# The expert layers of a streaming encoder: half of u and all values written as a software pipeline that three engines keep in program order

## The chip, the cores and the metric

One core of one Trainium2 chip runs the whole program as one launch. The metric is the device time of that launch in microseconds (us). Before the change it is 2491.96 us, the median of 3 runs (2488.18 to 2493.15).

Names of engines: TensorE (PE in the profile, its weight loads PEld), VectorE (DVE), ScalarE (ACT), GpSimd (POOL), and SyncE (SP), which only issues loads here.

## The reference

The program is one step of an encoder with two layers, a state-space mixer and an attention mixer, each followed by the same kind of expert layer ("peer"). There are 256 prompt rows and 8 x 16 = 128 sample rows. The change touches the expert layer alone, which runs twice:

```python
def peer(xn, w_q, sub_k1, sub_k2, u_tab, v_tab):
    ...
        vs, ci = lax.top_k(cand, PEER_TOPK)
        e1 = jnp.take_along_axis(i1, ci // PEER_TOPK, axis=-1)
        e2 = jnp.take_along_axis(i2, ci % PEER_TOPK, axis=-1)
        eid = (e1 * PEER_NKEYS + e2).reshape(PEER_TOKEN_BLOCK, PEER_HEADS * PEER_TOPK)
        gate = jax.nn.softmax(vs.astype(jnp.float32), axis=-1).reshape(PEER_TOKEN_BLOCK, PEER_HEADS * PEER_TOPK)
        ue = jnp.take(u_tab, eid, axis=0)
        act = jax.nn.gelu(jnp.einsum('tkd,td->tk', ue, xb).astype(jnp.float32))
        ve = jnp.take(v_tab, eid, axis=0)
        return jnp.einsum('tk,tkd->td', (gate * act).astype(xb.dtype), ve)
```

The table has 128 x 128 = 16384 experts of 1024 numbers each, u and v. A row picks 8 x 16 = 128 of them, with a gate for each.

## The kernel before

**Prompt rows, dense.** The 256 prompt rows use the whole table. The experts are cut into 128 blocks of 128, and a loop runs over blocks twice: first all of u, then all of v ("values"). The results of u are kept in two tiles, G[0] (blocks 0 to 63) and G[1] (blocks 64 to 127), as gelu(u x). Between u and values each entry of G is multiplied by its gate, or by zero.

**One step of u** (`u_step`) loads a block of 512 KB (tile `raw`), splits it into a rounded part `hi` (ScalarE, L111) and a rest `lo` (VectorE, L112), makes 24 matmuls of 256 columns (8 slices of the contraction times hi*xhi, hi*xlo, lo*xhi, L147 to L149), and takes the gelu of the bank on ScalarE. In the first half some blocks skip the split and are multiplied in full precision; in the second half (steps 64 to 127, the part that the change touches) none does.

**One step of values** (`v_step`) loads and splits a block of v in the same way, splits the slice of G into `phi` and `plo`, and makes 12 matmuls of 512 columns (L160): 2 row blocks, 2 halves, and hi*phi, lo*phi, hi*plo. 12 of the first 64 steps ("native": 3, 8, 13 up to 58) multiply the raw block by G itself (L1292). All 128 steps add into four banks.

**Gates** (`w_step`) make the gate matrix of 8 rows of tokens and one half of the experts: VectorE builds two one-hot tiles and scales one (`ob` L1258, `og` L1261, `oa` L1274), ScalarE builds the other `oa` (L1271, L1272), 16 small matmuls join them in a bank (L1278), and VectorE multiplies G by the bank (L1280). 32 such steps treat G[0] during the second half of u, and 32 treat G[1] during the first half of values; each stands at every second step.

**Sample rows, gathered.** The 128 sample rows use gathered rows of the table instead. GpSimd gathers 512 KB for each of 128 u items (L1139 into `gath`, three buffers, two items ahead), and VectorE multiplies and sums each (`u_item`, L1179). Their number by the step is set by the table `U_DUE`. For v, three sample groups of four are summed on TensorE: 24 "quads", each of four gathered tiles in a free part of G, a small tile `cm` from VectorE (L1230), and 8 matmuls in source, 16 in the trace (L1236); `V_DUE` sets their steps: 6 during u, 10 in the first half of values, 8 in the second. The fourth group is summed by VectorE, 32 items (L1204, `I_DUE`), in values.

**What sets the order.** Nothing in the expert layer is ordered by hand, but for instructions marked by `pin`, which keep their order among themselves (u items, quads). The framework's scheduler works out the order of all others for each engine from its own model of the durations and from the order in which the code records them. Each engine then runs its own list strictly in that order, and waits at an instruction whose inputs or buffers aren't ready.

**Buffers.** `raw` has 4. `hi` and `lo` have 2 in the second half of u and 3 in values, until the last few steps (2). `phi` and `plo` have 3. TensorE's 8 banks: 2 hold the sample sums, 4 the prompt sums (values only).

## Time and profile before

| what | before |
|---|---|
| median of 3 runs | 2491.96 us |
| the profiled execution | 2509.09 us |
| its span, first to last instruction | 2507.4 us |
| granted TensorE clock, mean | 0.986 |
| ScalarE, VectorE, GpSimd busy share | 50%, 78%, 30% |
| HBM read | 630.62 MB |

The profiled execution is some 0.7% slower than the median, so a difference that is worked out from the trace is scaled by 2491.96/2509.09. "Idle before" in a row is how long the engine waited just before that instruction, with what ended the wait. Matmuls overlap: one of 512 columns is shown with 0.40 us, but the next starts 0.23 us after it, so times of TensorE are read from start to start. A few per cent of its records are missing (a group of 48 may show 42).

### The profile page before, as it was taken

What the parts mean: (1) busy time and instruction counts of PE and PEld (TensorE: products, weight loads), DVE (VectorE), ACT (ScalarE), POOL (GpSimd) and SP (SyncE); (2) the same over time, 40 slices, a digit from 0 to 9 for tenths busy, and PEclk for the clock granted to TensorE, in tenths of its full rate; (3) what the DMA queues carried; (4) which work ended last, traced back from release to release, by engine and by line L of the source; (5) the groups of instructions that cost most, each with busy time, mean ns of one, the idle gap of its engine ahead of it and who ended that gap; (6) DMA issues with size and microseconds to landing.
All of it is one profiled execution on the core that took longest, in us unless ns stands there. A gap on an engine that the chain in (4) does not pass through costs nothing.

```text
span 2507.4 us, 44188 instructions
## 1 busy us (share of the span) xinstructions
PE 2399.9 (96%) x16431; PEld 2022.1 (81%) x16432; DVE 1951.7 (78%) x4217; ACT 1241.9 (50%) x2406; POOL 741.3 (30%) x779
## 2 busy tenths in 40 slices
PE   8999999999999999998999998999999999998998
PEld 7899978999988886656776778999998886656776
DVE  5888846979887888868875676978987897878965
ACT  5655524433465665553444554433465565554443
POOL 2222200012323224455442100012334224456441
PEclk9999999999999999999999999999999999999999
DMA  5545434467789889999895424467789888999995
GB/s 196 178 172 197 147 127 150 144 224 272 267 305 329 289 292 345 339 345 376 335 364 188 137 81 153 148 214 256 270 307 337 286 296 330 334 369 367 333 364 203
DMA packets 177080, 649.75 MB, mean 259 GB/s; under 512 B 21136, under 2 KB 23040, under 8 KB 174208
## 3 DMA queue, kind: packets, MB, share of 16 engines
q1 hardware_dynamic: 99936, 365.85, 40.8%
q0 software_dynamic: 76928, 281.07, 31.2%
q8 instruction: 129, 2.11, 0.3%
q14 instruction: 87, 0.71, 0.1%
HBM read 630.62 MB, written 18.06 MB: 259 GB/s over the span
## 4 chain that ended last, share of the span: by engine, by line
PE 68%; DVE 6%; issue 4%; ACT 2%; DMA 2%; POOL 1%; another core or an unknown queue 1%; POOLq 0%; SPq 0%; DVEq 0%; ACTq 0%
PE bank L160 23%; PE bank L149 10%; PE bank L147 9%; PE bank L148 9%; PE bank L1236 4%; PE bank L1245 4%; PE bank L1292 3%; PE bank L1278 3%; DVE lo L112 2%; DVE gath L1179 1%; ACT hi L111 1%; DMA gath<-in_p_u,eidU 1%; DMA h<-hd 1%; POOL G L1139 1%
## 5 line engine op out<-in xcount | busy, mean ns | idle before, releaser
L111 ACT CAST hi<-raw 128x1024 fp32r<-128x1024 f32 (+1 forms) x479 | 496.9, 1040 | 535.2 <-PE bank L148 349.8
L112 DVE TENSOR_TENSOR lo<-raw,hi 128x1024 fp32r<-128x1024 f32 (+1 forms) x479 | 579.5, 1212 | 191.1 <-ACT hi L111 165.1
L1139 POOL DMA_INDIRECT gath<-in_p_u,eidU x256 | 317.4, 1240 | 898.5 <-DVE gath L1179 486.6
L149 PE MATMUL bank<-xhi,lo 128*128 128x256 f32 (+1 forms) x1344 | 405.0, 302 | 8.0 <-DVE lo L112 6.9
L147 PE MATMUL bank<-xhi,hi 128*128 128x256 f32 (+1 forms) x1344 | 403.6, 301 | 0.6 <-ACT hi L111 0.3
L148 PE MATMUL bank<-xlo,hi 128*128 128x256 f32 (+1 forms) x1344 | 397.5, 296 | 0.2 <-issue 0.2
L1139 POOL DMA_INDIRECT G<-in_p_v,eidT x192 | 214.8, 1119 | 198.8 <-PE bank L1236 138.4
L111 ACT CAST phi<-G 128x256 fp32r<-128x256 f32 x232 | 93.8, 405 | 360.7 <-PE bank L160 317.5
L149 PEld LDWEIGHTS bank<-xhi,lo 128*128 128x128 f32 x1344 | 254.6, 189 | 16.5 <-DVE lo L112 8.5
L147 PEld LDWEIGHTS bank<-xhi,hi 128*128 128x128 f32 x1344 | 254.7, 190 | 13.8 <-issue 5.7
L148 PEld LDWEIGHTS bank<-xlo,hi 128*128 128x128 f32 x1344 | 254.8, 190 | 1.0 <-issue 0.7
L147 PE MATMUL bank<-qhi,hi 128*128 128x256 f32 (+1 forms) x792 | 244.4, 309 | 8.9 <-ACT xf L935 7.3
L149 PE MATMUL bank<-qhi,lo 128*128 128x256 f32 (+1 forms) x792 | 239.0, 302 | 2.6 <-DVE lo L112 2.6
L148 PE MATMUL bank<-qlo,hi 128*128 128x256 f32 (+1 forms) x792 | 238.8, 302 | 0.0
L160 PE MATMUL bank<-lo,phi 128*128 128x512 f32 x640 | 206.5, 403 | 7.9 <-DVE lo L112 5.8
L160 PE MATMUL bank<-hi,phi 128*128 128x512 f32 x640 | 198.9, 409 | 12.1 <-ACT hi L111 8.9
L1271 ACT ACTIVATE oa<-ioh,e2T 128x128 f16<-128x128 f16 x512 | 163.3, 390 | 90.0 <-PE bank L1278 70.1
L160 PE MATMUL bank<-hi,plo 128*128 128x512 f32 x640 | 203.4, 398 | 0.2 <-issue 0.2
L112 DVE TENSOR_TENSOR plo<-G,phi 128x256 fp32r<-128x256 f32 x232 | 97.7, 422 | 103.0 <-PE bank L160 94.8
L160 PEld LDWEIGHTS bank<-hi,phi 128*128 128x128 f32 x640 | 117.4, 188 | 61.1 <-ACT hi L111 18.2
L1179 DVE SCALAR_TENSOR_TENSOR gath<-gath,xg 128x1024 f32<-128x1024 f32 x128 | 155.3, 1213 | 9.6 <-DMA gath<-in_p_u,eidU 9.5
L147 PEld LDWEIGHTS bank<-qhi,hi 128*128 128x128 f32 x792 | 151.4, 191 | 10.4 <-ACT xf L935 7.8
(371 smaller groups left out, 5045.3 us busy)
## 6 DMA issues: line engine op xcount, KB each, us to landing
raw<-in_u_t SPq DMA_DIRECT2D x256, 512.0 KB
raw<-in_p_v SPq DMA_DIRECT2D x256, 512.0 KB
raw<-in_w_in SPq DMA_DIRECT2D x32, 512.0 KB
raw<-in_p_w_q SPq DMA_DIRECT2D x32, 512.0 KB
raw<-in_w_z SPq DMA_DIRECT2D x16, 512.0 KB
s<-in_state_ssm SPq DMA_DIRECT2D x8, 1024.0 KB
out_sm_ssm<-s SPq DMA_DIRECT2D x8, 1024.0 KB
raw<-in_w_out SPq DMA_DIRECT2D x16, 512.0 KB
```

The lines of the kernel that those rows point to most:

```text
L111: act.copy(hi, raw)
L112: dve.tensor_tensor(lo, raw, hi32, op=OP.subtract)
L147: pe.matmul(ps, whi[:, s], xhi[:, k, c0:c1], start=(k == 0), stop=False)
L148: pe.matmul(ps, whi[:, s], xlo[:, k, c0:c1], start=False, stop=False)
L149: pe.matmul(ps, wlo[:, s], xhi[:, k, c0:c1], start=False, stop=(k == KD - 1))
L160: mm = pe.matmul(ps, x, w[:, hf * n:(hf + 1) * n], start=s_, stop=e_)
L1139: pool.indirect_dma_start(out=tile_, out_offset=None, in_=tab, in_offset=bass.IndirectOffsetOnAxis(ap=idx, axis=0))
L1179: pin(dve.scalar_tensor_tensor(tile_, tile_, 1.0, xg[g], op0=OP.mult, op1=OP.mult, accum_out=au[g][:, j:j + 1]))
L1236: pin(pe.matmul(out_s[hf][32 * q:32 * q + 32, :], cm[:, q], rows[q][:, hf * 512:hf * 512 + 512], start=(r == 0), stop=(r == 31), tile_posi ...
L1245: pe.matmul(ps, raw[:, k * P:(k + 1) * P], xf[:, k], start=(k == 0), stop=(k == KD - 1))
L1271: act.activation(a[:, i], ioh, AF.Square, scale=-1.0, bias=e2T[:, t, 0:1])
L1278: pe.matmul(ps[:, i0 + i], a[:, i], eg[:, i0 + i, j], start=(j == 0), stop=(j == 1))
```

## The change

The second half of u and all of values are recorded in another order, and the instructions of TensorE, VectorE and ScalarE that are recorded there are chained: each one must come after the one recorded before it on the same engine (`in_order`). Loads and gathers (SyncE and GpSimd) are not chained. Steps are taken apart: weights are split one step ahead in u and two in values, the gelu of a step is recorded behind the split of a later one, and a gate step is spread over three steps (prepare, matmuls, multiply). Gate steps start at steps 0, 1, 3, 5 and so on, at 61/32 steps from one to the next, up to 59 (`w_at`), in place of 1, 3, up to 63. `phi` and `plo` keep 3 buffers, one of them in another pool. The residual `h` is loaded back two steps earlier, and the extra `hi`/`lo` buffer is given up there. The numbers and kinds of instructions are the same.

```diff
+AHEAD = 2 * 64 - 8
...
+    @contextmanager
+    def in_order():
+
+        traced = nc.cur_bb.bb.instructions
+        n, last = len(traced), {}
+        for i in traced:
+            last[i.engine] = i
+        kind = mybir.DependencyInfo(mybir.DependencyClass.NoSync, mybir.DependencyReason.DATA)
+        yield
+        for i in traced[n:]:
+            if i.engine in HELD:
+                if i.engine in last:
+                    tc.add_manual_dep(i, last[i.engine].name, kind, reason="in order")
+                last[i.engine] = i
...
+            def w_apply(hf, t0, ones, eg):
+
+                ps = bank([P, 8, HE])
+                for i in range(8):
+                    for j in range(2):
+                        pe.matmul(ps[:, i], ones[i // 4][:, i % 4], eg[:, i, j], start=(j == 0), stop=(j == 1))
+                return hf, t0, ps
...
+            def v_acts(e2):
+
+                if e2 in NATIVE_V:
+                    return None
+                n = turn_of["v"] = (turn_of.get("v", -1) + 1) % 3
+                pl, bufs = (vpool, 2) if n else (one, 1)
...
+                return split(phi, plo, G[e2 // HE][:, e2 % HE])
...
+            w_at = {(61 * i) // 32: 8 * i for i in range(32)}
+            made, mult, gelu = [], [], []
+
+            def gates(hf, e2):
+                if made:
+                    mult.append(w_apply(*made.pop()))
...
+            wt = u_weights(HE)
+            held = in_order()
+            held.__enter__()
             for e2 in range(HE):
-                u_step(HE + e2)
-                tick(HE + e2)
-                if e2 % 2 == 1:
-                    w_step(0, 8 * (e2 // 2))
+                if mult:
+                    w_mult(*mult.pop())
+                nxt = u_weights(HE + e2 + 1) if e2 < HE - 1 else v_weights(0)
+                if gelu:
+                    u_gelu(*gelu.pop())
+                if e2 == HE - 1:
+                    ph = v_acts(0)
+                gelu.append((HE + e2, u_products(HE + e2, wt)))
+                wt = nxt
+                gates(0, e2)
                 if e2 >= 7:
                     quads(HE + e2)
+                if e2 in w_at:
+                    made.append(w_prep(0, w_at[e2]))
+                tick(HE + e2)
+            u_gelu(*gelu.pop())
...
             for e2 in range(2 * HE):
-                v_step(e2)
+                if mult:
+                    w_mult(*mult.pop())
+                while n < 2 * HE and n <= e2 + (2 if n < AHEAD else 1):
+                    if n == AHEAD:
+                        more.clear()
+                    wt = v_weights(n)
+                    stage.append((wt, v_acts(n)))
+                    n += 1
+                v_products(e2, *stage.pop(0))
                 if e2 == 35:
                     load_group(3)
+                gates(1, e2)
+                quads(2 * HE + e2)
+                if e2 in w_at:
+                    made.append(w_prep(1, w_at[e2]))
                 tick(2 * HE + e2)
                 item_tick(2 * HE + e2)
-                if e2 < HE and e2 % 2 == 1:
-                    w_step(1, 8 * (e2 // 2))
-                quads(2 * HE + e2)
-                if e2 == 2 * HE - 7:
-                    more.clear()
+                if e2 == AHEAD - 1:
                     lent.__exit__(None, None, None)
                     h = open_h()
                     pool.dma_start(h, spill)
+            held.__exit__(None, None, None)
```

What moves on the engines is seen at three places of layer 0. The first is TensorE in values, about step 50, where a quad (`cm`) stands. Before:

```order
L1236 MATMUL bank_7299<-G_622_3973,cm_12474 32x512
L160 MATMUL bank_10553<-lo_12543,phi_12546 128x512
L160 MATMUL bank_10554<-lo_12543,phi_12546 128x512
L160 MATMUL bank_10553<-hi_12542,plo_12547 128x512
L160 MATMUL bank_10554<-hi_12542,plo_12547 128x512
L160 MATMUL bank_10555<-lo_12543,phi_12546 128x512
L160 MATMUL bank_10556<-lo_12543,phi_12546 128x512
L160 MATMUL bank_10555<-hi_12542,plo_12547 128x512
L160 MATMUL bank_10556<-hi_12542,plo_12547 128x512
L1236 MATMUL bank_7299<-G_622_3973,cm_12474 32x512
L1236 MATMUL bank_7300<-G_622_3973,cm_12474 32x512 x4
```

The same engine and place now, where L1309 are the gate matmuls (L1278 before), L1253 the quad and L177 the products:

```order
L1309 MATMUL bank_12533<-og_12501,oa_12509 128x64
L1253 MATMUL bank_7299<-G_622_3973,cm_12550 32x512 x4
L1253 MATMUL bank_7300<-G_622_3973,cm_12550 32x512 x4
L177 MATMUL bank_10583<-hi_12479,phi_12483 128x512
L177 MATMUL bank_10584<-hi_12479,phi_12483 128x512
```

Before, one quad was cut into pieces with products between them; now its 8 matmuls stand together behind a step's products and gate matmuls.

The second is VectorE about step 58 of values, near the end of the gate steps. Before:

```order
L1258 TENSOR_TENSOR ob_12578<-ioh_76,e1T_3965 128x512
L1280 SCALAR_TENSOR_TENSOR G_1195_7294<-bank_12508,G_1195_7294 128x64x8
L1261 TENSOR_TENSOR og_12580<-ob_12578,g_619_3967 128x1024
L1274 TENSOR_TENSOR oa_12596<-ioh_76,e2T_3966 128x512
L112 TENSOR_TENSOR lo_12701<-raw_12698,hi_12700 128x1024
L1258 TENSOR_TENSOR ob_12657<-ioh_76,e1T_3965 128x512
L1280 SCALAR_TENSOR_TENSOR G_1195_7294<-bank_12577,G_1195_7294 128x64x8
L1261 TENSOR_TENSOR og_12659<-ob_12657,g_619_3967 128x1024
L1274 TENSOR_TENSOR oa_12675<-ioh_76,e2T_3966 128x512
```

Now (L129 is `split`, L1315 the multiply, L1282 to L1300 the preparation, L1196 the u item, L1221 the v item, L1247 the small tile of a quad):

```order
L1315 SCALAR_TENSOR_TENSOR G_1195_7294<-bank_12691,G_1195_7294 128x64x8
L129 TENSOR_TENSOR lox_12714<-raw_12711,hix_12713 128x1024
L129 TENSOR_TENSOR plo_12718<-G_622_3973,phi_12717 128x256
L1247 SCALAR_TENSOR_TENSOR cm_12733<-iob_74,a_10196 128x128
L1282 TENSOR_TENSOR ob_12745<-ioh_76,e1T_3965 128x512
L1285 TENSOR_TENSOR og_12747<-ob_12745,g_619_3967 128x1024
L1300 TENSOR_TENSOR oa_12755<-ioh_76,e2T_3966 128x512
L1196 SCALAR_TENSOR_TENSOR gath_12633,au_12246<-gath_12633,G_622_3973 128x1024
L1221 SCALAR_TENSOR_TENSOR G_622_3973<-G_622_3973,cU_3964 128x1024
```

Before, gate steps that had been put off followed each other with few splits between them; now each step holds at most one gate step's preparation and one multiply, behind the split of the weights.

The third is ScalarE in the second half of values. Before:

```order
L111 CAST phi_13247<-G_1195_7294 128x256
L111 CAST hi_13243<-raw_13241 128x1024
L111 CAST phi_13274<-G_1195_7294 128x256
L111 CAST phi_13299<-G_1195_7294 128x256
L111 CAST hix_13270<-raw_13268 128x1024
L111 CAST phi_13326<-G_1195_7294 128x256
```

Now:

```order
L128 CAST phi_13220<-G_1195_7294 128x256
L128 CAST hi_13241<-raw_13239 128x1024
L128 CAST phi_13245<-G_1195_7294 128x256
L128 CAST hi_13263<-raw_13261 128x1024
L128 CAST phi_13267<-G_1195_7294 128x256
L128 CAST hix_13290<-raw_13288 128x1024
```

Before, two or three `phi` of later steps stood ahead of the `hi` of a nearer one; now `hi` and `phi` of the same step take turns, `hi` first.

More of the change, by code (lines that the diff above doesn't have):

```diff
@@ L26 @@
 NSEQ = 8
+HELD = (mybir.EngineType.PE, mybir.EngineType.DVE, mybir.EngineType.Activation)
 TS = 16
@@ L1275, in w_step, with w_mult @@
                                           e2T[:, ts].unsqueeze(2).to_broadcast([P, 4, P // 2, 2]), op=OP.is_equal)
[L1276 to L1278 removed]
+                return hf, t0, ones, eg
+            def w_apply(hf, t0, ones, eg):
[4 more added lines that the diff above has]
+                return hf, t0, ps
+            def w_mult(hf, t0, ps):
                 gv = G[hf][:, :, t0:t0 + 8]
```

50 lines of the change are left out of this document (29 added, 21 removed).

## The prediction

> **What bounds the kernel now.** I read the page first, then the work by stage, then the chain of work that ended last, and the timeline where TensorE waits.
>
> ```profile
> PE 2399.9 (96%) x16431; PEld 2022.1 (81%) x16432; DVE 1951.7 (78%) x4217; ACT 1241.9 (50%) x2406; POOL 741.3 (30%) x779
> ```
>
> TensorE looks full, but matmuls overlap, so 96% doesn't say how far it is from its own rate. The timeline of TensorE gives the stages of layer 0:
>
> ```profile
> 678.96 0.28 PE L147 MATMUL bank<-xhi,hi 128*128 128x256 f32 x1
> ...
> 679.32 0.28 PE L147 MATMUL bank<-xhi,hi 128*128 128x256 f32 x1
> ...
> 907.47 0.28 PE L149 MATMUL bank<-xhi,lo 128*128 128x256 f32 x1
> 909.35 0.73 PE L160 MATMUL bank<-hi,phi 128*128 128x512 f32 x2 [1.60 <-ACT phi L111]
> ...
> 1366.61 0.27 PE L208 MATMUL bank<-ident,oT 128*128 128x128 f32 x1
> ```
>
> The second half of u, the first work that reads `xhi`, begins at 678.96. Values begin at 909.35, after a wait of 1.60 for `phi`, and the attention's first transpose at 1366.61 ends them: 230.4 and 457.3 us. Three matmuls of u take 0.36, so a step's 24 take 24 x 0.119 = 2.86. The chain has the other prices:
>
> ```profile
> 1046.33 0.48 PE bank L1278 x16
> 1046.81 1.85 PE bank L1236 x16
> ...
> 1055.02 3.43 PE bank L1292 x8
> ...
> 1277.51 11.32 PE bank L160 x48
> 1290.68 11.33 PE bank L160 x48
> ```
>
> A gate step's matmuls take 0.48. A whole quad takes 1.85, a native step 3.43. Four steps of values (48 matmuls) take 11.33, of which the last matmul's tail is 0.17: 2.79 a step. From 1277.51 to 1290.68 are 13.17, four steps and a quad, so a quad between such products costs 13.17 - 4 x 2.79 = 2.0; I take 1.95.
>
> So TensorE's own work is:
> - u: 64 x 2.86 + 32 x 0.48 + 6 x 1.86 + 0.8 for two small sums = 210.2 of 230.4.
> - values, first 44 steps (to the end of the ninth native, 1055.02 + 3.43 = 1058.45): 35 x 2.79 + 9 x 3.43 + 22 x 0.48 + 6 x 1.95 = 150.8. They took 149.1, because the scheduler had run only four of the six quads due.
> - values, last 84 steps: 81 x 2.79 + 3 x 3.43 + 10 x 0.48 + 12 x 1.95 + 2.8 = 267.3 (the 2.8 are the sample items' sum and one small sum). They took 308.2.
>
> TensorE bounds all three, and stands still for about 20, none and 41 us a layer. Where the 41 go is seen on VectorE and TensorE:
>
> ```profile
> 1114.25 0.68 DVE L1261 TENSOR_TENSOR og<-ob,g 128x1024 f16<-128x1024 f16 x1
> 1114.85 0.42 DVE L1274 TENSOR_TENSOR oa<-ioh,e2T 128x512 f16<-128x512 f16 x1
> 1115.18 1.22 DVE L112 TENSOR_TENSOR lo<-raw,hi 128x1024 fp32r<-128x1024 f32 x1
> 1116.32 0.42 DVE L1258 TENSOR_TENSOR ob<-ioh,e1T 128x512 f16<-128x512 f16 x1
> 1116.65 0.68 DVE L1280 SCALAR_TENSOR_TENSOR G<-bank,G 128x512 f32<-128x512 f32 x1
> 1117.25 0.68 DVE L1261 TENSOR_TENSOR og<-ob,g 128x1024 f16<-128x1024 f16 x1
> ...
> 1129.04 0.69 DVE L1280 SCALAR_TENSOR_TENSOR G<-bank,G 128x512 f32<-128x512 f32 x1 [3.14 <-PE bank L1236]
> ```
>
> Gate steps are crowded here, one every 3 us, just before G[1] is needed: TensorE and VectorE wait for each other in turn. A split quad costs too:
>
> ```profile
> 1092.58 1.04 PE L1236 MATMUL bank<-G,cm 128*32 128x512 f32 x2
> 1093.56 0.64 PE L1278 MATMUL bank<-og,oa 128*128 128x64 f16 x16
> 1094.13 1.04 PE L1236 MATMUL bank<-G,cm 128*32 128x512 f32 x2
> ```
>
> An eighth of a quad takes 1.0, over half of a whole one. And behind the gates a pattern comes back every 12.7 us:
>
> ```profile
> 1191.49 10.01 PE bank L160 x42
> ...
> 1201.53 0.41 ACT phi L111
> 1201.93 0.96 ACT hi L111
> ...
> 1202.91 1.24 DVE lo L112
> ...
> 1204.19 10.02 PE bank L160 x42
> ```
>
> ScalarE stood at a `phi` that needs the buffer of a running step, with the next step's `hi` queued behind it. So four steps take 12.7 for 11.2 of work.
>
> **The change part by part.** The instructions are the same, so only waits go or come.
>
> *u.* VectorE must keep up in its fixed order. Start to start, from the rows above and these:
>
> ```profile
> 1182.34 1.22 DVE L1179 SCALAR_TENSOR_TENSOR gath<-gath,G 128x1024 f32<-128x1024 f32 x1
> 1183.48 0.08 DVE L1179 DVE_READ_ACCUMULATOR gath<-gath,G 128x1 f32 x1
> 1183.48 1.28 DVE L1204 SCALAR_TENSOR_TENSOR G<-G,cU 128x1024 f32<-128x1024 f32 x1
> 1184.68 1.22 DVE L112 TENSOR_TENSOR lo<-raw,hi 128x1024 fp32r<-128x1024 f32 x1
> ```
>
> `lo` costs 1.14, a u item 1.14, a v item 1.20, and a gate step 0.33 + 0.60 + 0.33 + 0.60 = 1.86. In two steps of u (two `lo`, one gate step, 1.44 items by `U_DUE`) that is 2.28 + 1.86 + 1.64 = 5.8, against 2 x 2.86 + 0.48 = 6.2 on TensorE, more with quads. `lo` of the next step can start when ScalarE's `hi` ends, about 1.0 after the step begins (0.96 in the chain), and ends at 2.2 to 2.6; it is needed at 2.86 or later. So it is hidden, with half a microsecond to spare. The gate matmuls come a step after their preparation and find it done. The boundary's 1.60 goes, since the first `phi` is made in u's last step.
>
> What comes in its place: a quad waits for `cm`, which now stands in the same step behind that step's `lo`. At best it is ready when the products end; behind an item of the step before it is up to 1 us late. Between 0 and 1.0 for each quad, I take 0.4, nearer to the first because half of the quads stand behind gate matmuls: 2.4 in u. I add 3 for small waits, the size of the largest that TensorE has in this stage now:
>
> ```profile
> PE bank L1278 <- ACT oa L1272: 3.2, 2, 1.6
> ```
>
> So u: 210.2 + 2.4 + 3 = 215.6, a gain of 14.8.
>
> *Values, first 44 steps.* In two steps VectorE has 5.9 (1.48 x 1.82 for `lo` and `plo`, 1.86, 1.19 items), against 6.2 to 7.2 on TensorE with two steps of lead. All six quads are now done: 150.8 + 6 x 0.4 = 153.2, a loss of 4.1.
>
> *Values, last 84 steps.* The crowd of gates, the split quads and the `phi` pattern go. Late next are the DMAs. The stretches:
>
> ```profile
> 909.35:1057.00 147.65, 147.65 (x842) 100.86 (x843) 121.51 (x206) 82.93 (x164) 63.83 (x55) 1.00 0.90 328
> 1057.00:1150.00 93.00, 82.27 (x528) 49.56 (x526) 65.81 (x111) 42.46 (x93) 52.26 (x46) 0.96 0.93 356
> 1150.00:1245.00 95.00, 86.27 (x363) 66.62 (x364) 87.06 (x118) 42.47 (x62) 46.26 (x32) 1.00 0.94 352
> ...
> 1140.00:1150.00 10.00, 7.25 (x28) 4.65 (x26) 7.70 (x10) 2.79 (x5) 5.35 (x5) 1.00 1.02 410
> ...
> 1180.00:1190.00 10.00, 10.00 (x44) 8.11 (x44) 9.82 (x14) 3.77 (x7) 4.65 (x4) 1.00 1.00 361
> ```
>
> The columns are length, busy times of the five engines, clock, DMA share and GB/s. With DMA engines all busy they carry 361 to 410. Steps 44 to 63 need 20 blocks, 12 u rows, about 18 v rows for quads and 9 for items, of 0.524 MB each: 31 MB, or 76 us at 410 and 86 at 361. TensorE's work there is 17 x 2.79 + 10.3 + 4.8 + 4 x 1.95 = 70.3. I take 5 more for it, with 410 as the end that the packed stretch 1140 to 1150 shows, and keep 0 to 15. In steps 64 to 87 VectorE has 1.48 + 0.75 x 1.14 + 0.48 x 1.20 = 2.91 a step against 2.79, and 24 blocks, 18 u rows and 11 or 12 items in 70 us ask for 400 GB/s: 5 more (3 to 12). With 2.8 for `cm` and 2 at the end, where `hi` has two buffers, 267.3 + 14.8 = 282: a gain of 26.
>
> *Sum.* 14.8 - 4.1 + 26 = 37 a layer. Layer 1 runs the same code, so 74 in all: 2509.09 - 74 = 2435, and at the median 2435 x 2491.96/2509.09 = **2419 us**.
>
> A rule of the Trainium skill speaks against the middle of this. "DMA: Bandwidth & Descriptors", section "Where 436 GB/s comes from", holds that loads from HBM are bound at about 358 GB/s a core. By it the stretch from 1057 to 1245, now at 352 to 356, could not shrink, and the sum would be that of the second rival below. The trace doesn't agree over short stretches: 410 in the row from 1140.
>
> **The rivals.**
>
> *Nothing is late* (6%): every wait goes, TensorE's own work is left, 210.2 + 150.8 + 267.3 = 628.3 of 687.7 a layer. That is 119 in all, 2374. Against it: DMA at 0.93 to 0.94 busy already.
>
> *DMA or the small tile takes the gain of values* (21%): if the stretches at 352 and 356 keep their length, 188 us, values gain nothing, and u 14: 28 in all, 2464. Or `cm` costs 1.0 for all 24 quads, 14 more than I took, beside the 86 us for 31 MB, 11 more: 12 a layer are left, 2468. With both, a few more: 2455 to 2480.
>
> *A late gather holds VectorE* (13%, slower). Place: the u item now stands in VectorE's fixed list with the next `lo` behind it, and TensorE behind that. One gather in the chain took 9.5 to land:
>
> ```profile
> 1141.05 9.52 DMA gath<-in_p_u,eidU
> ```
>
> The lead is three items, some 13 us, less GpSimd's own wait at a gather for a quad. In u VectorE has 230.4/32 = 7.2 in two steps before the stage gets longer than it was, and needs 5.8: so it decides from 1.4/1.44 = 1.0 us of wait an item. At 1.5, u takes 32 x 7.96 = 255, the first 44 steps 22 x 7.7 = 169, and the rest gains 5 less: 25 + 20 - 21 = 24 slower a layer, 2540. Against it: the program order of items and gathers is as before, and VectorE now waits 0.4 in all for them in u:
>
> ```profile
> DVE gath L1179 <- DMA gath<-in_p_u,eidU: 0.4, 1, 0.4
> ```
>
> *No change* (5%): the waits come back elsewhere in the same size, as when `hi` of step n+2 waits for its buffer longer than two steps of lead. That the order isn't what the code says is excluded by the rows of the change.
>
> **How the numbers follow.** The forecast with its bounds, 2395 to 2450, has 55%, and with the rivals above the range 2380 to 2480 holds about 8 in 10. Its low end takes in most of the case that nothing is late, its high end the DMA and `cm` case; left out are no change and slower. A measurement of this kernel tells about 0.2% (5 us) from no change. Faster 0.82, the same 0.05, slower 0.13.
>
> **What would show it.** In the changed profile u should take about 216 and values about 435 a layer, quads stand whole at 1.85 to 2.2, gate multiplies 6 to 7 us apart to the end, and no `phi` row on ScalarE stand ahead of a wait of TensorE. TensorE's waits should be for VectorE's `cm` and for weights in steps 44 to 88, with DMA share near 1. Wrong it would be if VectorE shows long waits for `gath`, if ScalarE waits for `raw` by several microseconds, or if u stays near 230.

## The result, and the profile after

| | before | after |
|---|---|---|
| median, us | 2493.15 (5 runs, 2488.18 to 2495.15) | 2474.88 (5 runs, 2471.26 to 2483.6) |
| profiled execution, its span | 2509.09, 2507.4 | 2483.6, 2481.9 |

The ratio is 0.9937, with a 95% interval of 0.9914 to 0.9959: faster by 18 us or 0.6%, clear of the scatter, but a quarter of the 73 that were forecast at the median. The busy shares of the engines hardly differ from those of before (TensorE 96%, VectorE 79%, ScalarE 49%, GpSimd 31%).

The stages of layer 0 stand in the timeline of TensorE (start, duration, engine, line, operation, tiles, shape, count). Here L164 to L166 are the products of u, L177 those of values, L225 the attention's first transpose:

```profile
684.73 0.28 PE L164 MATMUL bank<-xhi,hi 128*128 128x256 f32 x1
...
901.39 0.62 PE L177 MATMUL bank<-hi,phi 128*128 128x512 f32 x2
...
1350.05 0.63 PE L177 MATMUL bank<-lo,phi 128*128 128x512 f32 x2
1350.51 0.63 PE L177 MATMUL bank<-hi,plo 128*128 128x512 f32 x2
1350.98 0.27 PE L225 MATMUL bank<-ident,oT 128*128 128x128 f32 x1
```

The second half of u takes 901.39 - 684.73 = 216.7 where it took 230.4. Values are counted here to the start of the last product that reads `phi`, the second of the row at 1350.05: 448.9 (456.6 before, by the same rule). So by these two profiles u did what was forecast, and values didn't. For u they mislead: when both kernels are profiled in one group of runs, its gain is about half of that (see the experiments). TensorE's waits in the values of layer 0, by what ended them, before and after:

```profile
PE bank L160 <- ACT hi L111: 4.9, 5, 1.0
PE bank L1278 <- DVE og L1261: 3.9, 2, 2.5
PE bank L160 <- DVE lo L112: 3.0, 4, 1.0
PE bank L1278 <- ACT oa L1272: 2.6, 2, 1.9
```

```profile
PE bank L1182 <- DVE cm L1203: 4.9, 1, 4.9
PE bank L177 <- DVE lo L129: 3.8, 5, 1.9
PE bank L1253 <- DMA G<-in_p_v,eidT: 3.3, 2, 2.6
PE bank L1253 <- DVE cm L1247: 2.9, 4, 1.3
```

Columns are the sum, the number and the longest. The waits of before for `hi`, `og` and `oa` are gone. New are those for a sum of a sample group (L1182, `group_end`) and, at the quads (L1253), for gathered rows of v (`G`) and for `cm`; those for `lo` were there before, but have other causes now. Each has its place. First the rows, TensorE around steps 33 to 38:

```profile
1013.43 3.59 PE L1342 MATMUL bank<-raw,G 128*128 128x512 f32 x8
...
1031.67 1.04 PE L1253 MATMUL bank<-G,cm 128*32 128x512 f32 x2
1035.31 1.05 PE L1253 MATMUL bank<-G,cm 128*32 128x512 f32 x4 [2.60 <-DMA G<-in_p_v,eidT]
1037.07 3.50 PE L1253 MATMUL bank<-G,cm 128*32 128x512 f32 x10 [0.71 <-DMA G<-in_p_v,eidT]
1040.50 0.70 PE L1342 MATMUL bank<-raw,G 128*128 128x512 f32 x1
```

L1342 is a native step. From step 33 to step 38 are 27.1 us, for a native step, four others, three gate steps and two quads: 3.43 + 4 x 2.79 + 1.44 + 3.9 = 19.9 by the prices of the prediction. The quad of step 37 starts, stops and waits, and its last ten matmuls take 3.4 us where a whole quad of 16 takes 1.85. Its rows were asked for after the quad of step 33, which ended at 1019.3. The chain has the last of them, issued at 1025.81 and landed 11.22 later:

```profile
1025.81 11.22 DMA G<-in_p_v,eidT
```

Then VectorE at about step 69. L1196 is the u item, L129 the split:

```profile
1147.00 1.23 DVE L1196 SCALAR_TENSOR_TENSOR gath<-gath,G 128x1024 f32<-128x1024 f32 x1 [4.77 <-DMA gath<-in_p_u,eidU]
...
1148.15 1.22 DVE L129 TENSOR_TENSOR lo<-raw,hi 128x1024 fp32r<-128x1024 f32 x1
```

VectorE stands 4.77 us at a row of u that has not landed, and `lo`, whose inputs are there, stands behind it in the fixed list. TensorE at the same place:

```profile
1149.42 1.14 PE L177 MATMUL bank<-lo,phi 128*128 128x512 f32 x2 [1.90 <-DVE lo L129]
1150.36 1.05 PE L177 MATMUL bank<-hi,plo 128*128 128x512 f32 x2
1151.21 1.05 PE L177 MATMUL bank<-hi,phi 128*128 128x512 f32 x2
...
1152.92 0.65 PE L177 MATMUL bank<-hi,plo 128*128 128x512 f32 x2
1153.41 0.63 PE L177 MATMUL bank<-hi,phi 128*128 128x512 f32 x2
```

The wait is 1.90, and behind it two matmuls take 0.85 to 0.94 from start to start where they take 0.46 to 0.49 otherwise: TensorE runs at half rate for 3.5 us (the granted clock is 0.52 from 1149.4 to 1152.9), so the late row costs about twice its wait. Last the group sum, on TensorE and on VectorE, at step 88:

```profile
1215.03 1.88 PE L1182 MATMUL bank<-ident,cm 128*128 128x32 f32 x8 [4.86 <-DVE cm L1203]
```

```profile
1214.59 0.29 DVE L1203 TENSOR_TENSOR cm<-au,same_q 128x128 f32<-128x128 f32 x1
1217.18 0.19 DVE L1187 TENSOR_TENSOR a<-a,gT 128x32 f32<-128x32 f32 x1 [2.30 <-ACT a L1185]
```

TensorE's fixed list has the sum right behind the products of the step in which the last u item is recorded, but VectorE gets to that item and to the sum's input only 4.9 later. Then VectorE waits in its turn, 2.30, for ScalarE's gelu of the sum, and the granted clock is 0.50 from 1215 to 1220.

The work by stretch shows how full the loads are where u rows are late (length, busy times of PE, PEld, DVE, ACT, POOL, then clock, DMA share, GB/s). The four stretches run from step 44 to the end of values:

```profile
1063.00:1113.00 50.00, 49.92 (x318) 33.57 (x317) 41.49 (x68) 26.32 (x56) 32.21 (x28) 1.00 1.02 407
1113.00:1163.00 50.00, 45.59 (x216) 33.56 (x215) 41.17 (x60) 20.84 (x34) 29.13 (x24) 0.97 1.02 402
1163.00:1210.00 47.00, 45.85 (x194) 35.77 (x192) 47.00 (x66) 21.49 (x32) 28.02 (x20) 1.00 1.01 395
1210.00:1350.00 140.00, 133.65 (x629) 95.66 (x629) 86.66 (x118) 54.12 (x85) 38.45 (x37) 0.98 0.80 289
```

From step 44 to 88 the loads run at 395 to 407 GB/s for 147 us with a DMA share over 1, and behind that at 289. Counted from the ninth native step to the first product of step 88, these steps take 153.2 and 153.8 us in the two layers, where they took 176.9 and 175.8 before: here lies the gain of values. The loads come close to the 410 that the trace of before showed over 10 us.

### The profile page after: what moved, and what is told of

The parts are those of the page before. It is cut to its first block, busy times and chain, and to the rows that moved or that the text cites. A ratio compares the mean times of both kernels' runs of the same rounds, so it can differ in the third digit from the quotient of the medians.

```text
span 2481.9 us, 44016 instructions
## 1 busy us (share of the span) xinstructions
PE 2388.1 (96%) x16432; PEld 2026.9 (82%) x16432; DVE 1952.8 (79%) x4217; ACT 1227.7 (49%) x2406; POOL 771.7 (31%) x779
## 4 chain that ended last, share of the span: by engine, by line
PE 59%; DVE 9%; DMA 7%; issue 5%; POOL 2%; ACT 2%; POOLq 0%; SPq 0%; DVEq 0%; ACTq 0%
PE bank L177 17%; PE bank L164 9%; PE bank L166 9%; PE bank L165 9%; PE bank L1253 4%; DMA G<-in_p_v,eidT 3%; PE bank L1267 3%; PE bank L1342 3%; DVE lo L129 2%; PE bank L1309 2%; DVE gath L1196 2%; DMA gath<-in_p_u,eidU 2%; DMA raw<-in_u_t 1%; POOL G L1156 1%; ACT hi L128 1%
## 5 line engine op out<-in xcount | busy, mean ns | idle before, releaser
L129 DVE TENSOR_TENSOR lo<-raw,hi 128x1024 fp32r<-128x1024 f32 (+1 forms) x479 | 579.3, 1210 | 222.9 <-ACT hi L128 221.6
L1156 POOL DMA_INDIRECT gath<-in_p_u,eidU x256 | 344.5, 1346 | 845.2 <-DVE gath L1196 409.1
L164 PE MATMUL bank<-xhi,hi 128*128 128x256 f32 (+1 forms) x1344 | 407.8, 304 | 0.0
L166 PE MATMUL bank<-xhi,lo 128*128 128x256 f32 (+1 forms) x1344 | 399.6, 297 | 5.8 <-DVE lo L129 5.8
L1156 POOL DMA_INDIRECT G<-in_p_v,eidT x192 | 220.0, 1146 | 209.4 <-PE bank L1253 125.9
L164 PEld LDWEIGHTS bank<-xhi,hi 128*128 128x128 f32 x1344 | 255.2, 190 | 14.2 <-issue 7.8
L166 PEld LDWEIGHTS bank<-xhi,lo 128*128 128x128 f32 x1344 | 254.9, 190 | 8.0 <-DVE lo L129 7.8
L164 PE MATMUL bank<-qhi,hi 128*128 128x256 f32 (+1 forms) x792 | 245.6, 311 | 8.8 <-ACT xf L952 7.2
L166 PE MATMUL bank<-qhi,lo 128*128 128x256 f32 (+1 forms) x792 | 239.5, 303 | 3.8 <-DVE lo L129 3.8
L177 PE MATMUL bank<-lo,phi 128*128 128x512 f32 x640 | 203.7, 399 | 8.9 <-DVE lo L129 8.9
L177 PE MATMUL bank<-hi,phi 128*128 128x512 f32 x640 | 209.8, 409 | 0.1
L177 PE MATMUL bank<-hi,plo 128*128 128x512 f32 x640 | 202.0, 397 | 0.0
L128 ACT CAST hix<-raw 128x1024 fp32r<-128x1024 f32 x97 | 101.4, 1046 | 166.0 <-PE bank L177 88.1
L1196 DVE SCALAR_TENSOR_TENSOR gath<-gath,G 128x1024 f32<-128x1024 f32 x128 | 155.9, 1218 | 19.1 <-DMA gath<-in_p_u,eidU 19.1
L1196 DVE SCALAR_TENSOR_TENSOR gath<-gath,xg 128x1024 f32<-128x1024 f32 x128 | 155.1, 1215 | 9.4 <-DMA gath<-in_p_u,eidU 9.3
L164 PEld LDWEIGHTS bank<-qhi,hi 128*128 128x128 f32 x792 | 152.0, 192 | 10.3 <-ACT xf L952 7.7
L177 PEld LDWEIGHTS bank<-hi,phi 128*128 128x128 f32 x640 | 116.0, 189 | 49.9 <-issue 15.3
```

The costliest lines, as they stand in the source:

```text
L128: act.copy(hi, raw)
L129: dve.tensor_tensor(lo, raw, hi32, op=OP.subtract)
L164: pe.matmul(ps, whi[:, s], xhi[:, k, c0:c1], start=(k == 0), stop=False)
L166: pe.matmul(ps, wlo[:, s], xhi[:, k, c0:c1], start=False, stop=(k == KD - 1))
L177: mm = pe.matmul(ps, x, w[:, hf * n:(hf + 1) * n], start=s_, stop=e_)
L1156: pool.indirect_dma_start(out=tile_, out_offset=None, in_=tab, in_offset=bass.IndirectOffsetOnAxis(ap=idx, axis=0))
```

## The experiments

Each ran beside the kernel before, on one chip for a group of runs: e1 to e4, e5 to e8, e9 to e12, e13 to e15 and e16 to e18. Ratios are to before in the same group, with the 95% interval. u and values are read as above, from the first product with `xhi` to the first of values, and from there to the start of the last product that reads `phi`, for layer 0 and 1.

| run | u | values | ratio |
|---|---|---|---|
| after | 216.7, 217.4 | 448.9, 449.2 | 0.9937 (0.9914 to 0.9959) |
| e1 order in u alone | 216.9, 217.2 | 463.2, 463.8 | 1.0040 (1.0022 to 1.0059) |
| e2 group sum later | 216.6, 217.5 | 442.4, 440.2 | 0.9866 (0.9839 to 0.9893) |
| e3 `cm` earlier | 216.9, 217.2 | 448.8, 446.8 | 0.9889 (0.9866 to 0.9912) |
| e4 more lead for rows | 217.1, 217.7 | 446.0, 445.7 | 0.9877 (0.9851 to 0.9903) |
| e5 without v rows in values | 223.6, 225.8 | 434.5, 434.6 | 0.9836 (0.9805 to 0.9868) |
| e6 the three edits | 224.5, 224.4 | 436.6, 437.2 | 0.9842 (0.9811 to 0.9872) |
| e7 one row a step | 224.3, 222.4 | 449.2, 449.7 | 0.9937 (0.9909 to 0.9964) |
| e8 u items earlier | 222.3, 224.7 | 446.7, 445.5 | 0.9895 (0.9862 to 0.9928) |
| e9 before again | 228.3, 229.8 | 459.2, 459.3 | |
| e10 after again | 222.2, 224.3 | 449.6, 450.9 | 0.9936 (0.9913 to 0.9960) |
| e11 order in values alone | 234.8, 237.0 | 455.9, 450.7 | 1.0051 (1.0030 to 1.0072) |
| e12 three, slower u items | 224.4, 223.9 | 437.8, 437.5 | 0.9837 (0.9818 to 0.9855) |
| e13 last rows from step 76 | 217.4, 218.0 | 446.7, 448.1 | 0.9942 (0.9928 to 0.9957) |
| e14 three, last rows from 76 | 217.8, 216.7 | 437.1, 437.3 | 0.9840 (0.9823 to 0.9858) |
| e15 without v rows in u | 216.7, 216.7 | 446.9, 446.7 | 0.9938 (0.9913 to 0.9963) |
| e16 load moved behind step 78 | 221.7, 221.7 | 446.1, 445.2 | 0.9875 (0.9854 to 0.9895) |
| e17 three, load moved | 223.5, 222.8 | 427.0, 426.3 | 0.9771 (0.9751 to 0.9791) |
| e18 before again | 227.0, 225.6 | 456.4, 454.3 | |

A single edit moves a ratio by about as much as the rest of the program varies: between the layers 444 to 454 us were found among these profiles. The profiled execution of e3, for one, is 15 below that of after, and some 13 of them lie ahead of u and between the layers, which the edit doesn't touch. So single edits are judged by the stage that they touch.

**Is it the order that does it?** e1 ends `in_order` ahead of values, e11 begins it there.

> Only the second half of u keeps the fixed order; values are recorded in the new order, but the scheduler arranges them. In the changed kernel u took 216.7 and 217.4 us, values 448.9 and 449.2, the whole 2474.9; before the change values took 456.6 and 454.9. Theory 1 (the fixed order of values is worth its gain of 6 to 8 a layer, and it is held back by its own waits): values go back to about 455 to 457, u stays at 217, the whole about 2488. Theory 2 (values are bound by their loads, whatever the order): values 447 to 451, the whole 2473 to 2477. Theory 3 (the order held by hand costs more than it brings, since the scheduler had put the group sum and the quads off without a stall): values under 445, the whole under 2467.

```diff
             u_gelu(*gelu.pop())
+            held.__exit__(None, None, None)
             xpool.__exit__(None, None, None)
...
-            held.__exit__(None, None, None)
```

> Only values keep the fixed order; the second half of u is recorded in the new order, but the scheduler arranges it. Theory 1 (it is the fixed order that shortens u): u as in the kernel before on this chip. Theory 2 (the new order of recording does it alone, the scheduler follows it): u within 2 of the changed kernel's. Values within 2 of the changed kernel's by both.

```diff
-            held = in_order()
-            held.__enter__()
             for e2 in range(HE):
...
             u_gelu(*gelu.pop())
+            held = in_order()
+            held.__enter__()
             xpool.__exit__(None, None, None)
```

Without the order, values take 463 (e1; 4 to 9.5 longer than in the profiles of before, which come from other groups of runs) and u takes 236 (e11; 7 longer than in e9 on the same chip). The scheduler does worse with the new way of recording than with the old one. The order itself takes 14.5 from values and 12.6 from u, and about half of that only makes up for this. In e1 theory 1 had the direction, but not the size: the whole became slower than before the change. In e11 u is longer than by either theory, nearer to theory 1. Its values were to stay within 2 of e10's by both; in layer 1 they do, in layer 0 they take 455.9 for 449.6. TensorE waits 8.7 for `cm` there, 3.4 in e10; why is not known.

**Which waits are lost time?** Three edits, each for one of the waits in the table.

> The sum of the last sample group (in the trace a wait of 5.3 us on TensorE at step 88 of values) stands two steps later, and VectorE's multiply behind it one step later still. Theory 1 (a fixed order waits where it was written, and the wait is lost time): the wait goes, values 449 to about 444, the whole 2465. Theory 2 (the loads bound the values): the time comes back as waits for weights in steps 88 to 100, values within 2 of 449, the whole 2473 to 2477.

```diff
-                a4 = a.rearrange("p (c r) -> p c r", r=RG)
+                late.append(g)
+
+            late = []
+
+            def group_mult():
+                g = late.pop()
+                a4 = coef[g].rearrange("p (c r) -> p c r", r=RG)
                 dve.tensor_tensor(a4, a4, group(gT, g), op=OP.mult)
...
-                if due and done["u"] == P:
+                        group_mult()
+                if late:
+                    group_mult()
+                if due and done["u"] == P and s >= U_DUE[-1][0] + 2:
```

> The small tile cm of a quad is made at the head of the quad's step, ahead of that step's lo, in place of behind it. In the changed kernel TensorE's waits for cm are 0.2 to 1.7 a quad. Theory 1 (TensorE waits for cm in the fixed order, about 0.4 a quad as the prediction had it): u 2 shorter, values 7 shorter, the whole about 2457. Theory 2 (the 0.4 is hidden or taken up by the next wait): u and values within 2 of 217 and 449, the whole 2472 to 2477.

```diff
+                if e2 >= 7:
+                    cm_due(HE + e2)
...
             for e2 in range(2 * HE):
+                cm_due(2 * HE + e2)
                 if mult:
                     w_mult(*mult.pop())
```

> The ten quads of the first half of values stand at steps 20, 25, 30, 36, 42, 46, 50, 54, 59, 64 in place of 20, 24, 28, 33, 37, 42, 46, 50, 55, 59, so that their rows are asked for one to two steps earlier while only four buffers are free. In the changed kernel steps 33 to 38 took 27.1 us for 20 of TensorE's work, with waits for the gathered rows. Theory 1 (the lead of the rows is too short, and that is lost time): steps 33 to 38 go to about 21, values to about 443, the whole 2462. Theory 2 (the loads bound this stretch): the same time is lost in steps 38 to 64 in its place, values 447 to 451, the whole 2472 to 2477.

```diff
-V_DUE = [77 + 6 * i for i in range(6)] + [148 + int(4.4 * i) for i in range(10)] + [220 + 4 * i for i in range(8)]
+V_DUE = [77 + 6 * i for i in range(6)] + [148, 153, 158, 164, 170, 174, 178, 182, 187, 192] + [220 + 4 * i for i in range(8)]
```

e2: values are 6.5 and 9.0 shorter, and 7.0 and 7.2 of that lie in the last 84 steps, where the sum stands. That is more than the wait of 4.9, since the half rate behind it goes as well. Theory 1 holds. e3: 0.1 and 2.4; the waits for `cm` shrink from 2.9 to 1.9, and those for `lo` grow from 3.8 to 6.0. Theory 2 holds for the stage. e4: 2.9 and 3.5, half of what theory 1 asked. Its first 44 steps fall from 162.1 to 152.7 in both layers, of which some 2 are a quad that now stands behind them; the steps behind them grow by 6.5 and 5.9. Its waits show where that went:

```profile
PE bank L177 <- DVE lo L129: 7.4, 4, 5.5
PE bank L1253 <- DVE cm L1247: 5.3, 6, 2.4
```

No wait for rows is left, but `lo` waits 7.4 in place of 3.8 and `cm` 5.3 in place of 2.9. More than half of what was won at step 37 was lost again behind step 44.

**Loads, or the order's own waits?**

> Leaves out 72 of the 96 gathered rows of v a layer (those asked for during values): the quads multiply whatever stands in those parts of G, so the sample rows come out wrong, and all instructions of TensorE, VectorE and ScalarE stay. 37.7 MB a layer are not loaded and GpSimd issues 72 gathers fewer. Theory 1 (what values lose is mostly late gathers and a crowded memory): besides the 3.6 of waits for these rows, the waits for lo behind late u items and the slow stretch from step 44 go too; left are TensorE's own 418, about 5 for cm and 5 for the group sum: values 426 to 434, the whole about 2440. Theory 2 (the fixed order's waits between engines are the loss, memory only shows where it was late by chance): values 444 to 446, the whole about 2466.

```diff
-                vrows[n] = (half, e), gather(tile_, t_in["p_v"], eidT[:, 32 * q + r:32 * q + r + 1])
+                vrows[n] = (half, e), tile_ if s >= 2 * HE else gather(tile_, t_in["p_v"], eidT[:, 32 * q + r:32 * q + r + 1])
```

Values take 434.5, near theory 1's upper end and 10 below theory 2's. The stretches of this kernel:

```profile
1060.00:1110.00 50.00, 49.48 (x301) 32.64 (x300) 41.77 (x69) 28.57 (x59) 15.17 (x14) 1.00 0.84 290
1110.00:1150.00 40.00, 38.09 (x198) 29.14 (x197) 37.93 (x55) 17.34 (x28) 24.49 (x17) 1.00 0.94 356
1150.00:1200.00 50.00, 47.25 (x202) 37.42 (x200) 49.77 (x70) 22.66 (x34) 29.81 (x20) 1.00 1.01 397
```

At 290 and 356 GB/s no u row is late, and at 397 one, by 0.2 us. A rate near 400 alone doesn't make the rows late, then. Leaving out rows also frees GpSimd of 72 gathers, so e5 can't tell a lighter load from a shorter list on GpSimd.

> The three edits together: last group sum two steps later, cm at the head of its step, more lead for the rows. One by one they took 6.5, 0.1 and 2.9 from values of layer 0 and 9.0, 2.4 and 3.5 from layer 1. Theory 1 (separate losses, which add up): values 439 and 434, the whole about 2450. Theory 2 (what one edit frees is lost to the next late gather, so they don't add): values 442 and 440 as with the late group sum alone, the whole about 2461. Theory 3 (each wait hid another, so together they bring more): under 434 in both layers.

The three edits together give 436.6 and 437.2: 12 less than after on average, where one by one they took 9.5 and 14.9. They add up, as theory 1 says. The first 44 steps take 151.3 and 151.4, with five quads in place of six. What TensorE still waits for:

```profile
PE bank L177 <- DVE lo L129: 8.5, 6, 3.8
PE bank L1270 <- DVE cm L1253: 1.6, 2, 1.1
```

So what is left is `lo` behind late u rows. Seven runs looked for their cause; three of them turned out to ask nothing.

> From step 36 of values on one row of v is asked for in each step, in place of up to two, so that the four gathers of a quad do not stand in a row on GpSimd ahead of the next u item's gather. Theory 1 (bursts of v rows make the u items late, VectorE waits at the item, lo and TensorE behind it): waits for lo fall from 4.6 to under 2 in layer 0, values 444, the whole 2465. Theory 2 (the load as a whole is late, not the order of the gathers): values 447 to 451; if the rows become late in their turn, TensorE waits for G in steps 40 to 64 and values are over 451.

```diff
-                for _ in range(2):
+                for _ in range(2 if s < 2 * HE + 36 else 1):
```

> The u items of values are set by (128, 72), (172, 101), (192, 110) in place of (128, 72), (192, 110): 29 items in the first 44 steps in place of 26, and 9 in steps 44 to 63 in place of 12. Theory 1 (steps 44 to 63 are bound by their loads, 1.6 MB less at 400 GB/s is 4 us): values 445, the whole 2466. Theory 2 (the late items come from the lead of three buffers, not from the load): values 448 to 451, with new waits for lo in the first 44 steps.

```diff
-U_DUE = ((64, 30), (71, 31), (128, 72), (192, 110), (216, P))
+U_DUE = ((64, 30), (71, 31), (128, 72), (172, 101), (192, 110), (216, P))
```

> The three edits and other steps for the u items of values: (128, 72), (172, 102), (192, 114), so 30 in the first 44 steps, 12 in the next 20, and 14 in place of 18 in steps 64 to 87, where the three edits together still left 9.5 of waits for lo behind late u items in layer 0. Theory 1 (three buffers give too short a lead at 0.75 items a step, and 0.58 is slow enough): these waits fall under 4, values about 431, the whole 10 below that of the three edits, ratio to before about 0.980. Theory 2 (the load delays the rows at any spacing): values within 2 of 437, ratio 0.984.

```diff
-U_DUE = ((64, 30), (71, 31), (128, 72), (192, 110), (216, P))
+U_DUE = ((64, 30), (71, 31), (128, 72), (172, 102), (192, 114), (216, P))
```

> The changed kernel with one edit: the rows of the eight quads of steps 92 to 120 are asked for from step 76 on, in place of as soon as buffers come free, from step 59. Two buffers' worth, eight rows or 4.2 MB, leave the stretch in which u rows land late (14 to 16 us after their gather in the trace of the four edits). Theory 1 (rows asked for long ahead of their use crowd out the u rows that VectorE needs next): waits for lo in steps 60 to 88 of values go from 4.4 to under 1.5, values 445 to 443 and the whole 2 x 5 shorter: ratio to before 0.989 to 0.990. Theory 2 (the lead of three buffers is too short whatever else is loaded): values 448 to 451, ratio 0.9935.

```diff
-                last = 4 * V_FIRST if s < 2 * HE else 4 * len(QR)
+                last = 4 * V_FIRST if s < 2 * HE else 4 * V_FIRST + 40 if s < 2 * HE + 76 else 4 * len(QR)
```

> The three edits (last group sum two steps later, cm at the head of its step, more lead for rows in the first half) with the rows of the last eight quads held back to step 76. Theory 1: the 9.5 of waits for lo that the three left in layer 0 fall under 3, values 430, ratio to before 0.979. Theory 2: values 436 to 438 as with the three alone, ratio 0.984.

e7, e13 and e14 asked nothing. GpSimd isn't chained: the scheduler still arranges its list, and asks for a row of v as soon as its buffer is free, whatever the step in which the code records it. In all three the instructions of every engine came out in the order of the kernel without the edit. In the trace of e13 as in that of after, eight rows for the last quads are asked for some 205 to 227 us into values. So e7 and e13 are the changed kernel again (0.9937, 0.9942), and e14 is e6 again (0.9840 for 0.9842). What they give is the scatter of a measurement, and one more thing: values of 449 and 447, 437 and 437 agree between groups of runs whose u differs by 7.

So theory 1 of e7 and of e13, that rows of v stand on GpSimd ahead of the next u row's gather, stays untested. The trace of after speaks for it. VectorE frees a buffer of u rows at 1126.1, and GpSimd asks for the next row 5.1 later, behind four rows of v:

```profile
1126.03 0.08 DVE L1196 DVE_READ_ACCUMULATOR gath<-gath,G 128x1 f32 x1
```

```profile
1124.34 1.11 POOL L1156 DMA_INDIRECT G<-in_p_v,eidT  x1 [1.96 <-PE bank L1253]
...
1128.63 1.60 POOL L1156 DMA_INDIRECT G<-in_p_v,eidT  x1 [0.47 <-issue]
1131.19 0.93 POOL L1156 DMA_INDIRECT gath<-in_p_u,eidU  x1 [0.96 <-DMA gath<-in_p_u,eidU]
```

There are three buffers, so this is the row of the third item on, the one that VectorE stood at for 4.77 up to 1147.00, 15.8 after its gather. Had it been asked for at once and landed as fast, it would have come about in time (an estimate from these rows). So a row is late by its place on GpSimd and by its landing, and no run here parts the two.

The other two did change the lists. e8 takes 2 to 4 from values, about what three rows less in steps 44 to 63 are worth (1.6 MB, 4 us). But its steps 44 to 88 take 152.6 and 151.5, and those of after, e7, e10 and e13, one and the same kernel, 152.4 to 158.4, so its cause isn't settled. e12 has 14 u items for 18 in steps 64 to 87, and values of 437.8 for 437: theory 2, the pace isn't the cause. It asks for four rows of u less from step 44 on than e6 (25 for 29 in 147 us, 5 us at 400 GB/s), and yet steps 44 to 88 take 153.3 and 154.1 for 153.6 and 154.3. The last pair moves more of the load out:

> The changed kernel with load moved out of steps 44 to 88 of values, which in its profile run at 395 to 407 GB/s for 147 us, while steps 88 to 128 run at 289: the 32 items of v that VectorE sums stand in steps 78 to 119 in place of 50 to 117 (about 10 fewer before step 88), and the rows of the last eight quads are asked for from step 86 on. About 18 rows, 9.4 MB or 23 us at 400 GB/s, leave the stretch. Theory 1 (the memory's rate bounds these steps): waits for lo behind late u items go under 1.5, the rate in the stretch falls under 390, values about 441, ratio to before 0.987. Theory 2 (the lead of three buffers makes the items late at any load): values 447 to 451, ratio 0.9935. A third way (VectorE, with 0.78 items a step behind step 88, becomes the bound there): the last 40 steps get longer than the 140 of the changed kernel.

```diff
-I_DUE = (178, 245)
+I_DUE = (206, 247)
...
-                last = 4 * V_FIRST if s < 2 * HE else 4 * len(QR)
+                last = 4 * V_FIRST if s < 2 * HE else 4 * V_FIRST + 40 if s < 2 * HE + 86 else 4 * len(QR)
```

> The three edits together with the moved load of the run ahead. Theory 1: what the three left to late u items (9.3 of waits in layer 0 and some 3 of half clock) goes, values 427 to 430, close to the 418 of TensorE's own work; ratio to before 0.977. Theory 2: values 436 to 438 as with the three alone, ratio 0.984.

Of the two parts of this edit only the first came about; the rows of the last quads were asked for as early as before, as in e13. So not 18 rows are moved, but the gathers of v items: in the 147 us from step 44 on, 13 are issued where it was 23 in after and 21 in e6. That is about 9 rows, 4.7 MB, 12 us at 400 GB/s. TensorE's waits in the values of layer 0, first in e16, then in e17:

```profile
PE bank L1182 <- DVE cm L1203: 5.8, 1, 5.8
PE bank L1253 <- DMA G<-in_p_v,eidT: 5.2, 4, 1.9
PE bank L1253 <- DVE cm L1247: 3.6, 5, 1.7
PE bank L177 <- DVE lo L129: 0.2, 1, 0.2
```

```profile
PE bank L177 <- DVE lo L129: 2.7, 3, 1.8
```

In e16 the waits for `lo` are gone, 0.2 for 3.8, as theory 1 says. Values are 3 and 4 shorter and not 8. Steps 44 to 88 gain 6.2 and 4.6, although the group sum waits 5.8 for 4.9; in layer 0 the rows of the early quads are later still, and the first 44 steps lose 3.5. With the three edits these waits are gone too: e17 has values of 427.0 and 426.3, 10.5 below the three edits alone and 9 above TensorE's own 418, as theory 1 had it. Its stretches from step 44 on:

```profile
1055.00:1105.00 50.00, 50.00 (x321) 34.18 (x320) 38.55 (x66) 26.93 (x56) 29.02 (x27) 1.00 1.02 402
1105.00:1155.00 50.00, 48.16 (x239) 34.65 (x238) 37.44 (x61) 21.47 (x35) 26.79 (x20) 0.98 0.99 390
1155.00:1195.00 40.00, 40.00 (x172) 32.48 (x171) 38.50 (x55) 18.99 (x28) 25.11 (x16) 0.99 0.98 364
1195.00:1330.00 135.00, 133.93 (x642) 95.62 (x641) 101.95 (x133) 55.46 (x86) 59.56 (x49) 1.00 0.91 351
```

Steps 44 to 88 take 143.2 and 141.9 for 153.6 and 154.3 in e6, about the time of the 9 rows at that rate. That moving these gathers brings it is shown. That the memory's rate does it, as theory 1 has it, is argued: the gathers leave GpSimd's list as well, and the four rows of e12 brought nothing. The load is level now, 402 falling to 351 where it was 407 falling to 289, and TensorE is busy nearly throughout. e17 beats both kernels: 2443.96 us, 2.3% under before (and the changed kernel is 0.6% under it).

**What is u worth?** In the groups of e5 to e12, u took 5 to 9 longer with the same order.

> The kernel before, unchanged, so that its stages and those of the next run come from one chip. In the first group of runs u with the fixed order took 216.6 to 217.7, in the second group 222.3 to 225.8 with the same order, so that chips differ by about 7 in this stage. Theory 1 (the gain in u is the 13.7 and 12.4 that the first two profiles show): u is 13 longer here than in the next run. Theory 2 (about half of that is a difference of chips, since the first profile of before shows the same kind of waits as the second group): u is 5 to 7 longer here than in the next run.

> The changed kernel, unchanged, beside the run ahead of it. Theory 1: u 13 shorter and values 7 shorter than in the run ahead. Theory 2: u 5 to 7 shorter, values 7 shorter. The stretches outside the second half of u and values should differ by under 3 in each layer if their difference in the first two profiles (5.5 between the layers) was one of runs; by 5 again if it comes from the changed order there.

On one chip u goes from 228.3 to 222.2 and from 229.8 to 224.3, 6 a layer: theory 2. Values go from 459.2 to 449.6 and from 459.3 to 450.9. Outside these stages the changed kernel is 6 slower in this pair (2.8 ahead of u, 1.2 between the layers, 2.4 at the end). So the 5.5 between the layers was a matter of runs. The end wasn't: it takes 9.0 in the three profiles of before, 11.7 in after and 11.4 in e10. The pair has a scatter of its own: e9 is a single execution of 2515.1, 10 above the median of its group, and the profiled one of e10 is 3 above its median.

> The changed kernel, leaving out 20 of the 24 gathered rows of v that are asked for during u (the quads multiply what an earlier row left there, so sample rows come out wrong). 10.5 MB a layer less in u, all instructions of TensorE, VectorE and ScalarE as before. The u of the first run of this group is the comparison. Theory 1 (what u takes beyond 216 on some chips is late loads): u is 215 to 217 here, whatever it is there. Theory 2 (the difference of chips lies in the engines, not in the loads): u within 1.5 of that of the first run, 222 to 224 if this is the slower kind of chip; on the quicker kind, 217, the two theories give the same.

> The kernel before, unchanged, beside the two. If this group is on the quicker kind of chip (u with the fixed order 217): by theory 1 u of before is 222 to 224 here, so that the order is worth 6 in u on both kinds; by theory 2 it is 229 to 231, so that it is worth 13 on this kind and 6 on the other. If the chip is of the other kind (u 222 to 226 in the two runs), it repeats 228 to 230.

e15 met a chip on which u takes 217 anyway, so its two theories can't be told apart. e18 has u of 227.0 and 225.6 beside 221.7 to 223.5 in e16 and e17, a gain of 3 to 5. What u of the kernel before takes where the changed one takes 217 was not measured. The ratio speaks for a gain as small there: after has 0.9937 in the first group and 0.9942 in e13, 0.9936 and 0.9937 where u takes 222 to 224. The kernel before as a whole is 11 to 15 us shorter in the former groups (2494 and 2490 for 2505; 2500 in the last group), and twice 7 in u would be 14. But its u there isn't shown.

## Why the prediction missed the size

The direction was right, and 2474.9 lies in the range, but in the second rival's part of it: a quarter of the forecast gain came. The pair e9 and e10, on one chip, gives the terms; the first 44 steps end with the ninth native step, as in the prediction:

| a layer | forecast gain | measured, layer 0 and 1 |
|---|---|---|
| u | 14.8 | 6.0, 5.5 |
| values, first 44 steps | -4.1 | -13.4, -10.6 |
| values, last 84 steps | 26 | 22.9, 19.0 |
| sum | 37 | 15.5, 13.9 |

The 29 of both layers aren't all in the medians of this group, which differ by 16: the other stages are 6 slower in the changed kernel, and the pair's two executions stand 10 and 3 above their medians. Of the 45 that are missing in these stages, u has 18, the first 44 steps 16 and the last 84 steps 10. The steps that failed are two terms put at nothing, the lead of the gathered rows and the last group sum, and one too small, the small waits of u.

**u.** The sum of 215.6 was met in the first profile (216.7), but not in the pair. The kernel before takes 228.3 and 229.8 there, close to the 230.4 from which the step went; the changed one takes 222.2 and 224.3. So it is the sum that failed on this chip: "3 for small waits" is 9.6 and 11.7 there. The trace of e10 has 4.4 of TensorE's waits in u of layer 0 for 1.0 in after. Why the same order takes 6 more there stays open.

**First 44 steps.** The step summed TensorE's work and 0.4 for each `cm`, and put the gathered rows at nothing. It did not ask how long before its quad a row can be asked for while there are four buffers: some four steps, 12 us. The last row of step 37 was asked for 6.5 after the quad of step 33 had ended, behind other gathers on GpSimd, and took 11.2 more. Steps 33 to 38 lost 7. Before the change the scheduler put two of the six quads off, and TensorE had no wait in these steps. e4 and e6 show that the lead was the cause: with more of it these steps take 151.3 in e6 with five quads, so about 153.3 with the sixth, where the sum had 153.2.

**Last 84 steps.** The sum is closest here. The crowd of gates and the `phi` pattern went, as forecast. What it had no term for is `group_end`: the scheduler had kept it off the path, and the fixed order put it on it, 7 us a layer in these steps (e2). The terms of 5 and 5 for the loads were of the right size: with the group sum out of the way, steps 44 to 88 take 146.2 and 146.5 (e2), where TensorE's work of 137.3, the 10 for the loads and 1.6 for `cm` make 148.9. They become too small when the steps ahead lose nothing: e6 takes 153.6 and 154.3, with one quad more. Moving 9 rows out of this stretch brought 10.5 of a layer there (e17 against e6). `cm`, 9.6 a layer in the sum, cost 0 to 2.4 (e3).

**The rivals.** The second one came out in its number alone. It held that the stretch at 352 to 356 GB/s keeps its length, or that `cm` costs 1.0 a quad; but steps 44 to 88 went from 177 to 153 at 395 to 407 GB/s, and `cm` cost 2.4 a layer at most (e3). That the time fell into its part of the range is luck: the lead of the rows, the group sum and u took the gain. The Trainium skill, "DMA: Bandwidth & Descriptors", section "Where 436 GB/s comes from", has loads from HBM bound at about 358; the 147 us at 395 to 407 don't agree. "Perfetto Trace Analysis" of the Trainium skill, section "Roofline", lets a core that is active alone pull more, up to about 435, and this trace agrees with it. The third rival, the late gather, is there in small: VectorE's waits for u rows in the values of layer 0 are 7.7 in four, for some 56 items, where it needed 1.0 an item to decide. "Nothing is late" was out of reach for this change, but e17 comes within 9 us a layer of it in values.

**The signs.** Of the list at the prediction's end, quads stand whole but for the one of step 37, and waits for `cm` came. Gate multiplies are 6 to 9 us apart in the main, with one gap of 15.7 behind step 37. Values are 449 for 435. The waits for weights were `lo` behind VectorE's waits for u rows. The sign against it, VectorE at `gath`, is in the trace, 7.7 in all.

## What to carry to other kernels

When the order of several engines is fixed, a late load stops every engine that stands behind its reader; so work out for each load how long before its reader it can be asked for, from the step that frees its buffer and from what stands ahead of it on the engine that issues it, and compare that with its landing time in the trace. Count the bytes asked for in each stretch of steps as well, and move what is not needed there to a stretch with room. See in the instruction lists that it did move: an engine that is left to the scheduler may take no notice of where the code records its loads. Everything the scheduler used to put off (a small sum, an early quad) needs a place a few steps behind its inputs in the fixed list. And take a stage's gain from two profiles of one chip, never from one profile and a sum.

## What the runs showed of the hardware

- A wait of TensorE can cost more than itself: behind the wait of 1.90 above, the granted clock was about 0.5 for 3.4 us. In the values of all 20 profiles, each of the 37 waits of over 3.2 us was followed by 3 to 7 us at a granted clock of 0.5, and of the 71 waits of 1.5 to 2.7 us 43 were, the others not. In after such stretches cost 6 to 7 us in the values of a layer.
- A gather of 512 KB that was issued in 1.2 us landed 11.2 us after its start while the DMA share was 1.0, and one in the chain of the changed kernel (at 1128.63) took 15.96.
- The same order of u took 216.6 to 218.0 in some groups of runs and 221.7 to 225.8 in others. In e10 ScalarE stands 4.70 us at a `hi` (at 780.60) for something that the profile does not name; in after it waits 2.22 at the same instruction for the buffer. `hi` reads `raw` alone, so a late load of weights is likely, but its cause stays open.
